# Where two modulation units stand beside the dense expert rows, and when their sums are taken

## The chip, the cores and the metric

The kernel runs on one core of one Trainium2 chip. Its time is the device time of that core in microseconds (us). Before the change three runs took 1870.52, 1871.92 and 1872.52 us, a median of 1871.92. A core has five engines that run side by side, each in the order of its own list of instructions: PE (matrix products), DVE (elementwise work on vectors), ACT (activations, copies and casts), POOL (here mostly the issue of gathers) and SP (here the issue of DMA transfers). They wait for one another by semaphores.

## The reference, cut to what matters

One layer over 512 tokens of 1024 values: a modulated norm, a token mixer, a second modulated norm, and a product-key mixture of 16384 experts (PEER).

```python
mod = (cond @ ada_w[l] + ada_b[l])[:, None, :]             # 6 vectors of 1024
sh1, sc1, gt1, sh2, sc2, gt2 = jnp.split(mod, 6, axis=-1)
...                                                        # token mixer, x = x + gt1 * y
h = rmsnorm(x, norm2_g[l]) * (1.0 + sc2) + sh2
x = x + gt2 * peer(h, peer_wq[l], peer_subkeys[l], peer_u[l], peer_v[l])
return rmsnorm(x, final_g)

# in peer, for each token: the 128 (expert, gate) pairs of its eight heads, then
ue = jnp.take(u_tab, experts, axis=0)
ve = jnp.take(v_tab, experts, axis=0)
act = jax.nn.gelu(jnp.einsum('pd,phkd->phk', xb, ue), approximate=False) * gate
return jnp.einsum('phk,phkd->pd', act, ve)
```

The last modulation vector, `gt2`, is used only at the very end, when the sum over the experts is scaled and added to x.

## The kernel before, in words

The modulation product is cut into 12 units of 512 output columns, two for each vector. `ada_unit(u)` loads the 1024 x 512 weights of one unit in four transfers of 512 KB (tile `adaw`), and DVE adds the eight row blocks, each times its 128 values of the condition, into `adac` (128 x 512, one operation at L152 and seven at L158). The sum over the 128 partitions is one PE product with a matrix of ones (L167), which takes one of the two PSUM banks named `hg`; DVE adds the bias row `adar` (loaded at L165) and a store sends the row to DRAM (`g2d`). Units 10 and 11 are the two halves of `gt2`.

The experts are computed in two ways. For 368 of the 512 tokens every expert is computed: this is the dense part, and it bounds the last half of the program. For the rest, 16 + 128 steps gather 1 MB of expert rows each by indirect DMA (POOL, L1175), and for each step DVE makes a dot product (L1188) and, after a small Gelu on ACT (L1192), an accumulation into `acc` or `accx` (L1183).

The dense part goes over 128 rows of 128 experts. Products are made in three passes of split numbers: a float32 tile `raw` of 512 KB is loaded, ACT casts its high part `whi` (L1020), DVE subtracts it to give the low part `wlo` (L1021), and PE makes lo x hi, hi x lo and hi x hi (L209 to L211).

- `scores(i)`: splits row i of u (`in_ut`), makes 24 products into a bank `hg`, and ACT takes the Gelu (L1034) into the ring `ga`. The first 32 rows are made earlier in the program and parked in DRAM; they come back as `gr`.
- `value_parts(i)`: splits row i of v (`in_uv`), multiplies `ga` or `gr` by the gates on DVE (L1156), casts the high part `ah` on ACT (L1158) and makes the low part `al` on DVE (L1159). `ah` and `al` have two buffers, for even and odd rows.
- `value_sum`: 18 products of row i into the accumulators `y`.

`dense()` runs over rows 0 to 125: the value part of row i, its 18 products, then from row 29 on `scores(i + 3)`, so that PE makes 18 products a row up to row 28, and 18 and 24 in turn after that. Behind rows 8 and 16 it calls `ada_unit`. The tiles `raw` and `adaw` share four buffers. `dense()` and `gather_all()` are generators that `run` advances in turn; from what they emit, a scheduler in the build sets the order of every engine by its own model of their times. At run time the engines keep that order.

Two tiles of a kind are told apart below by the number behind the name.

Of the kernel before, what the change touches and what calls it, by code (L numbers as in the profile page):

```python
# [68 lines left out]
def mixer_peer_kernel(ctx: ExitStack, tc: tile.TileContext, x, ws, ada, wba, vecs, rows, skt, uv, ut, out, dbg=None):  # L69
    nc = tc.nc  # L70
# [16 lines left out]
    def bank(tag):  # L87
        return (psh if tag == "hg" else ps).tile([P, 512], F32, tag=tag, name=tag, bufs=psb[tag])
# [4 lines left out]
    def w2(tag, shape=(P, 2, 256), dt=F32, bufs=1, name=None):  # L93
        pool = wka if tag in WKA else wkb if tag in WKB else wk
        return pool.tile(list(shape), dt, tag=tag, name=name or tag, bufs=bufs)
# [19 lines left out]
    ones = cst.tile([P, P], F32, name="ones")  # L115
# [21 lines left out]
    def ada_unit(u, first=False, pool=None):  # L137


        def work(name):  # L140
            return w2("ac", (P, 512), bufs=2, name=name) if pool is None else pool.tile([P, 512], F32, tag=name, name=name)

        pp = bank("tr") if pool is None else None
        acc = work("adac")
        parts = []
        for i in range(4):
            w = st.tile([P, 2, 512], F32, tag="raw", name="adaw")
            nc.sync.dma_start(w, ada[u, :, 2 * i:2 * i + 2])
            for a in range(2):
                kk = 2 * i + a  # L150
                if kk == 0:
                    nc.vector.tensor_scalar(acc, w[:, 0, :], cond[:, 0:1], None, op0=ALU.mult)  # L152
                elif first and a:
                    p = w2("gs", (P, 512), bufs=NGS, name="adap")
                    nc.scalar.mul(p, w[:, a, :], cond[:, kk:kk + 1])
                    parts.append(p)
                else:
                    nc.vector.scalar_tensor_tensor(acc, w[:, a, :], cond[:, kk:kk + 1], acc,  # L158
                                                   op0=ALU.mult, op1=ALU.add)
        parts.append(acc)  # L160
        if u // 2 in (2, 5):
            dst, o = (g1d, RW_B1) if u < 6 else (g2d, RW_B2)
            k = u % 2 * 512
            r = work("adar")
            nc.sync.dma_start(r, bass.AP(tensor=rows.tensor, offset=rows.offset + o + k, ap=[[0, P], [1, 512]]))  # L165
            pp = bank("hg") if pp is None else pp
            nc.tensor.matmul(pp, ones, acc, start=True, stop=True)  # L167
            nc.vector.tensor_add(r, r, pp)
            nc.sync.dma_start(dst[:, k:k + 512], r)
            return  # L170
        for n, p in enumerate(parts):
            for c in range(4):
                nc.tensor.matmul(pp[:, c * P:(c + 1) * P], p[:, c * P:(c + 1) * P], ones, start=n + c == 0,
                                 stop=n == len(parts) - 1, skip_group_check=True)
        m = mod[:, 4 * u:4 * u + 4]
        nc.vector.tensor_add(m, pp.rearrange("p (c n) -> p c n", c=4)[:, :, 0],
                             vec[:, VC_ADAB + 4 * u:VC_ADAB + 4 * u + 4])
        if u // 2 in (1, 4):
            dst, g = (a1, VC_N1) if u < 6 else (a2, VC_N2)
            k = u % 2 * 4  # L180
            nc.vector.scalar_tensor_tensor(dst[:, k:k + 4], m, 1.0, vec[:, g + k:g + k + 4], op0=ALU.add, op1=ALU.mult)
# [617 lines left out]
    def ada_rest():  # L799
        for u in range(4, 10):  # L800
            ada_unit(u)
            yield
# [128 lines left out]
    for u in (2, 0):  # L931
        ada_unit(u, True)
    for i in range(PRE):
        early[U_K, i] = half_unit(U_K, i)
    for u in (3, 1):
        ada_unit(u, True)
# [89 lines left out]
    def scores(i):  # L1026

        uh, ul = split_load(ut[i])
        o = bank("hg")
        for kk in range(KD):  # L1030
            c = slice(kk * P, (kk + 1) * P)
            mm3(o[:, :ND], uh[:, c], ul[:, c], dhi[:, kk, :], dlo[:, kk, :], kk == 0, kk == KD - 1)
        a = den.tile([P, ND], F32, tag="ga", name="ga", bufs=RING)
        nc.scalar.activation(a, o[:, :ND], AF.Gelu)  # L1034
        ga_ring[i] = a
# [86 lines left out]
    d3 = ctx.enter_context(tc.tile_pool(name="d3", bufs=1, **RT))  # L1122
# [19 lines left out]
    def value_parts(i):  # L1142
        vh, vl = split_load(uv[i * P:(i + 1) * P, D:2 * D])
        if i % 8 == 0:
            g = d3.tile([P, ND // 16, 8, 16], F32, tag="g", name="g", bufs=2)
            for b in range(GB if i == 0 else 1):
                q = slice(8 * b, min(8 * b + 8, ND // 16)) if i == 0 else slice(0, ND // 16)
                nc.sync.dma_start(g[:, q], gd[:, q, i:i + 8, :])
            gtile[0] = g
        if i < AHEAD:  # L1150
            a = den.tile([P, ND], F32, tag="gr", name="gr", bufs=BACK)
            nc.sync.dma_start(a, sd[i])
        else:
            a = ga_ring.pop(i)
        a3 = a.rearrange("p (q t) -> p q t", t=16)
        nc.vector.tensor_mul(a3, a3, gtile[0][:, :, i % 8, :])  # L1156
        ah, al = ahl[i % 2]
        nc.scalar.copy(ah[:, 0:ND], a)  # L1158
        last["lo"] = nc.vector.tensor_sub(al[:, 0:ND], a, ah[:, 0:ND])  # L1159
        return ah, al, vh, vl  # L1160

    def value_sum(i, b, hf, ah, al, vh, vl):
        c = slice(b * P, (b + 1) * P)
        d = slice(hf * 512, hf * 512 + 512)
        return mm3(yacc[b][:, d], ah[:, c], al[:, c], vh[:, d], vl[:, d], i == 0, i == P - 1)
# [49 lines left out]
    def dense():  # L1215
        for i in range(P - NEND):
            v = value_parts(i)
            for b in range(GB):
                for hf in range(2):
                    value_sum(i, b, hf, *v)  # L1220
            if AHEAD <= i + LEAD < P:
                scores(i + LEAD)
            if i in (8, 16):
                ada_unit(10 + i // 16, pool=d3)
            if i >= AHEAD - LEAD or i % 2:
                yield
            if i >= AHEAD - LEAD and i % 7 in (0, 2, 5):
                yield
# [14 lines left out]

    ga_ = gather_all()
    run(dense(), ga_)
    run(ga_)
    gf = d3.tile([P, 2 * D], F32, tag="rows", name="gf", bufs=NROWS)
# [66 lines left out]
```

## Time and profile before

| | |
|---|---|
| median of 3 runs | 1871.92 us |
| the profiled execution | 1871.05 us |
| its span, first to last instruction | 1869.3 us |
| granted TensorE clock, mean over the span | 0.990 of full |
| PE products | 1815.7 us busy, 97% |
| DVE | 1595.9 us busy, 85% |
| ACT | 934.9 us busy, 50% |
| POOL | 439.7 us busy, 24% |
| DMA | 473.63 MB, mean 253 GB/s |

The busy time of an engine is the time in which its instructions run; the span is that of the program. The rows further down come from four views: busy time by windows (each engine's busy us and number of instructions in a stretch, then the granted clock, the DMA engines' busy share and GB/s), sums of waits (which instruction waited for which, us in total, how often, the longest), and timelines of single engines (start, duration, instruction, tiles out and in; in brackets the idle time before it and what ended that). Instructions of one engine overlap a little, so the price of one in a row of several is the distance between two starts, not its printed duration.

### The profile page before, as it was taken

The page shows a single profiled execution, that of the slowest core. Times are in us where ns is not written, and L with a number is a line of the kernel's source. Part 1 is how long each engine was busy: PE and PEld are TensorE (multiplying, and loading weights), DVE is VectorE, ACT ScalarE, POOL GpSimd, SP SyncE. Part 2 cuts the span into 40 slices and gives each one's busy share as a digit, 9 for nine tenths or more (in the row PEclk, how much of TensorE's full clock was granted, in tenths as well). Part 3 has the DMA queues.
Part 4 walks back from the last instruction along what each step waited for, and adds up shares of the span by engine and source line. Part 5 has one row for each costly group of instructions (what it writes and reads, how often), then busy time and mean ns, then how long its engine had stood idle before and what let it go on. Part 6 is the DMA issues. An engine that isn't in the chain of part 4 may idle for free.

```text
span 1869.3 us, 31386 instructions
## 1 busy us (share of the span) xinstructions
PE 1815.7 (97%) x11421; PEld 1680.2 (90%) x11421; DVE 1595.9 (85%) x3478; ACT 934.9 (50%) x1735; POOL 439.7 (24%) x445
## 2 busy tenths in 40 slices
PE   7999989999999899999999999999999999999997
PEld 6999978999998899999877889889889889889886
DVE  6889966989999979999887768888888888888886
ACT  6778644676655677766433333333333333333332
POOL 1000000000000698887001112222212212122210
PEclk9999998999999999999999999999999999999999
DMA  9655744543355555666999969989998998999883
GB/s 317 183 182 186 230 143 133 177 132 94 117 168 173 171 183 200 219 219 254 325 337 332 351 230 352 337 306 349 340 334 307 351 345 308 343 333 327 327 304 113
DMA packets 161146, 473.63 MB, mean 253 GB/s; under 512 B 13280, under 2 KB 76896, under 8 KB 139616
## 3 DMA queue, kind: packets, MB, share of 16 engines
q1 hardware_dynamic: 140256, 320.63, 51.1%
q0 software_dynamic: 20736, 151.00, 21.2%
q8 instruction: 90, 1.47, 0.3%
q14 instruction: 64, 0.52, 0.1%
HBM read 436.18 MB, written 35.39 MB: 252 GB/s over the span
## 4 chain that ended last, share of the span: by engine, by line
PE 50%; DVE 1%; ACT 0%; issue 0%; DVEq 0%; POOLq 0%; POOL 0%; ACTq 0%
PE y L211 10%; PE y L210 10%; PE y L209 10%; PE hg L209 7%; PE hg L211 7%; PE hg L210 7%; DVE t L1212 0%; ACT ah L1158 0%; DVE al L1159 0%; DVE accx L1183 0%; DVE t L1205 0%; DVE t L1206 0%; DVE wlo L1021 0%; DVE rows L1188 0%; DVE gr L1156 0%
## 5 line engine op out<-in xcount | busy, mean ns | idle before, releaser
L1020 ACT CAST whi<-raw 128x1024 fp32r<-128x1024 f32 x256 | 267.2, 1045 | 260.3 <-PE y L211 231.4
L1021 DVE TENSOR_TENSOR wlo<-raw,whi 128x1024 fp32r<-128x1024 f32 x256 | 312.7, 1222 | 97.1 <-ACT whi L1020 96.9
L209 PE MATMUL hg<-dlo,whi 128*128 128x368 f32 x1024 | 339.7, 332 | 2.2 <-ACT ga L1034 2.2
L211 PE MATMUL hg<-dhi,whi 128*128 128x368 f32 x1024 | 338.8, 331 | 0.0
L210 PE MATMUL hg<-dhi,wlo 128*128 128x368 f32 x1024 | 338.4, 330 | 0.0
L1175 POOL DMA_INDIRECT rows<-in_uv,ei x128 | 168.4, 1315 | 595.1 <-DVE acc L1183 537.2
L211 PE MATMUL y<-whi,ah 128*128 128x512 f32 x768 | 305.7, 398 | 0.0
L210 PE MATMUL y<-whi,al 128*128 128x512 f32 x768 | 305.6, 398 | 0.1
L209 PE MATMUL y<-wlo,ah 128*128 128x512 f32 x768 | 298.1, 399 | 1.1 <-DVE wlo L1021 1.1
L1055 POOL TENSOR_SCALAR oj<-iof,tj 128x128 f32<-128x128 f32 x248 | 215.4, 885 | 42.3 <-PE gd L1068 30.2
L205 DVE TENSOR_TENSOR wlo<-raw,whi 128x1024 fp32r<-128x1024 f32 x160 | 194.8, 1219 | 33.5 <-ACT whi L204 33.4
L204 ACT CAST whi<-raw 128x1024 fp32r<-128x1024 f32 x160 | 167.3, 1048 | 91.7 <-PE pj L211 61.5
L209 PEld LDWEIGHTS hg<-dlo,whi 128*128 128x128 f32 x1024 | 192.3, 188 | 7.2 <-ACT ga L1034 2.5
L210 PEld LDWEIGHTS hg<-dhi,wlo 128*128 128x128 f32 x1024 | 192.5, 188 | 4.2
L1034 ACT ACTIVATE ga<-hg 128x368 f32<-128x368 f32 x128 | 60.8, 476 | 263.1 <-PE hg L211 256.4
L211 PEld LDWEIGHTS hg<-dhi,whi 128*128 128x128 f32 x1024 | 192.2, 188 | 0.0
L211 PEld LDWEIGHTS y<-whi,ah 128*128 128x128 f32 x768 | 145.4, 189 | 35.4
L209 PEld LDWEIGHTS y<-wlo,ah 128*128 128x128 f32 x768 | 144.9, 189 | 33.2 <-DVE wlo L1021 1.9
L210 PEld LDWEIGHTS y<-whi,al 128*128 128x128 f32 x768 | 145.5, 189 | 32.1 <-DVE al L1159 0.4
L1188 DVE SCALAR_TENSOR_TENSOR rows<-rows,h2g 128x1024 f32<-128x1024 f32 x128 | 153.1, 1218 | 0.0
L209 PE MATMUL pj<-wlo,hh 128*128 128x256 f32 x448 | 128.8, 287 | 4.8 <-ACT gsig L629 2.1
L211 PE MATMUL pj<-whi,hh 128*128 128x256 f32 x448 | 128.1, 286 | 0.0
(814 smaller groups left out, 3872.1 us busy)
## 6 DMA issues: line engine op xcount, KB each, us to landing
raw<-in_ws SPq DMA_DIRECT2D x160, 512.0 KB
raw<-in_ut SPq DMA_DIRECT2D x128, 512.0 KB
raw<-in_uv SPq DMA_DIRECT2D x128, 512.0 KB
adaw<-in_ada SPq DMA_DIRECT2D x48, 512.0 KB
gd<-stage SPq DMA_DIRECT2D x23, 1024.0 KB
g<-gd SPq DMA_DIRECT2D x15, 1472.0 KB
sd<-ga SPq DMA_DIRECT2D x32, 184.0 KB
gr<-sd SPq DMA_DIRECT2D x32, 184.0 KB
```

The source lines that it names most:

```text
L204: nc.scalar.copy(hi, w)
L205: nc.vector.tensor_sub(lo, w, hi)
L209: nc.tensor.matmul(o, lh, rl, start=start, stop=False, **kw)
L210: nc.tensor.matmul(o, ll, rh, start=False, stop=False, **kw)
L211: return nc.tensor.matmul(o, lh, rh, start=False, stop=stop, **kw)
L1020: nc.scalar.copy(hi, w)
L1021: nc.vector.tensor_sub(lo, w, hi)
L1034: nc.scalar.activation(a, o[:, :ND], AF.Gelu)
L1055: (nc.gpsimd if a < npool else nc.vector).tensor_scalar(oj4[:, a, :], iof, tj[:, t0 + a:t0 + a + 1], None, op0=ALU.is_equal)
L1175: nc.gpsimd.indirect_dma_start(out=r[c], out_offset=None, in_=uv, in_offset=bass.IndirectOffsetOnAxis(ap=ei[:, c:c + 1], axis=0))
L1188: dot = nc.vector.scalar_tensor_tensor(u, u, 1.0, h2, op0=ALU.mult, op1=ALU.mult, accum_out=s)
```

## The change

Units 10 and 11 are called behind dense rows 40 and 56 instead of 8 and 16. For these two units `ada_unit` no longer makes the sum over the partitions; it returns a function that does, and `dense()` calls that function four rows later, behind rows 44 and 60, with a bank taken there. The loads, the eight DVE operations and the sums are the same in kind and number.

```diff
             r = work("adar")
             nc.sync.dma_start(r, bass.AP(tensor=rows.tensor, offset=rows.offset + o + k, ap=[[0, P], [1, 512]]))
-            pp = bank("hg") if pp is None else pp
-            nc.tensor.matmul(pp, ones, acc, start=True, stop=True)
-            nc.vector.tensor_add(r, r, pp)
-            nc.sync.dma_start(dst[:, k:k + 512], r)
+
+            def sum_up(pp):
+                nc.tensor.matmul(pp, ones, acc, start=True, stop=True)
+                nc.vector.tensor_add(r, r, pp)
+                nc.sync.dma_start(dst[:, k:k + 512], r)
+
+            if pool is not None:
+                return sum_up
+            sum_up(pp)
             return
...
-            if i in (8, 16):
-                ada_unit(10 + i // 16, pool=d3)
+            if i in (40, 56):
+
+                sums = ada_unit(10 + i // 56, pool=d3)
+            if i in (44, 60):
+                sums(bank("hg"))
```

The scheduler sets the order anew. PE's list is the same but for the two sums, POOL's is the same, and ACT's, DVE's and SP's lists differ from about dense row 7 on. Line numbers from L167 on are five higher in the kernel after the change.

ACT before, around dense row 17. `whi_12446` is the high part of row 17's v; `gr_12450` and `gr_12487` are the factors of rows 17 and 18:

```order
L1158 CAST ah1_11845<-gr_12450 128x368
L1192 ACTIVATE gg__12478<-gs__12476 128x1
L1158 CAST ah0_11843<-gr_12487 128x368
L1020 CAST whi_12446<-raw_12444 128x1024
L1020 CAST whi_12483<-raw_12481 128x1024
```

ACT after the change, at the same place. `whi_12400` is the high part of row 17's v; `gr_12375` and `gr_12404` are the factors of rows 16 and 17:

```order
L1163 CAST ah1_11845<-gr_12336 128x368
L1025 CAST whi_12400<-raw_12398 128x1024
L1197 ACTIVATE gg__12364<-gs__12362 128x1
L1163 CAST ah0_11843<-gr_12375 128x368
L1025 CAST whi_12437<-raw_12435 128x1024
L1163 CAST ah1_11845<-gr_12404 128x368
```

The cast of row 17's v moved from behind the cast of row 18's factor to ahead of that of row 16's.

ACT before, around dense row 57. `whi_14835` is the high part of row 57's v, `whi_14786` that of row 59's u; `ga_14669` and `ga_14745` are the Gelus of rows 57 and 58:

```order
L1034 ACTIVATE ga_14669<-hg_14644 128x368
L1020 CAST whi_14786<-raw_14784 128x1024
L1192 ACTIVATE gg__14822<-gs__14820 128x1
L1192 ACTIVATE gg__14830<-gs__14828 128x1
L1020 CAST whi_14835<-raw_14833 128x1024
L1158 CAST ah1_11845<-ga_14669 128x368
L1034 ACTIVATE ga_14745<-hg_14720 128x368
```

ACT after the change, around dense row 57. `whi_14831` is the high part of row 57's v; `ga_14722` and `ga_14792` are the Gelus of rows 58 and 59:

```order
L1039 ACTIVATE ga_14722<-hg_14697 128x368
L1163 CAST ah0_11843<-ga_14722 128x368
L1197 ACTIVATE gg__14962<-gs__14960 128x1
L1197 ACTIVATE gg__14970<-gs__14968 128x1
L1039 ACTIVATE ga_14792<-hg_14767 128x368
L1025 CAST whi_14831<-raw_14829 128x1024
L1025 CAST whi_14858<-raw_14856 128x1024
```

The cast of row 57's v moved from ahead of row 58's Gelu to behind row 59's. In PE's list, before and after alike, the 24 products of row 59's scores (`hg_14767` after) stand directly ahead of the 18 products of row 57.

DVE before, around dense row 57. `ga_14669` is row 57's factor, `wlo_14836` the low part of row 57's v, `wlo_14787` that of row 59's u:

```order
L1156 TENSOR_TENSOR ga_14669<-ga_14669,g_14761 128x368
L1021 TENSOR_TENSOR wlo_14787<-raw_14784,whi_14786 128x1024
L1193 TENSOR_TENSOR gg__14822<-gg__14822,gate_10666 128x1
L1193 TENSOR_TENSOR gg__14830<-gg__14830,gate_10666 128x1
L1183 SCALAR_TENSOR_TENSOR acc_13193<-rows_14671,gg__14822,acc_13193 128x1024
L1183 SCALAR_TENSOR_TENSOR acc_13193<-rows_14679,gg__14830,acc_13193 128x1024
L1021 TENSOR_TENSOR wlo_14836<-raw_14833,whi_14835 128x1024
L1159 TENSOR_TENSOR al1_11846<-ga_14669,ah1_11845 128x368
```

DVE after the change, around dense row 57. `ga_14792` is row 59's factor, `wlo_14832` the low part of row 57's v:

```order
L1161 TENSOR_TENSOR ga_14792<-ga_14792,g_14738 128x368
L158 SCALAR_TENSOR_TENSOR adac_14794<-adaw_14807,cond_104,adac_14794 128x512
L1188 SCALAR_TENSOR_TENSOR acc_13147<-rows_14813,gg__14962,acc_13147 128x1024
L158 SCALAR_TENSOR_TENSOR adac_14794<-adaw_14807,cond_104,adac_14794 128x512
L1188 SCALAR_TENSOR_TENSOR acc_13147<-rows_14821,gg__14970,acc_13147 128x1024
L1026 TENSOR_TENSOR wlo_14832<-raw_14829,whi_14831 128x1024
L1026 TENSOR_TENSOR wlo_14859<-raw_14856,whi_14858 128x1024
```

Ahead of the subtraction for row 57 there now stand row 59's factor and the last two `adac` operations of the second unit, with two accumulations between them.

DVE before, around dense row 41. `wlo_13715` is the low part of row 44's u, `ga_13597` row 42's factor:

```order
L1159 TENSOR_TENSOR al1_11846<-ga_13529,ah1_11845 128x368
L1188 SCALAR_TENSOR_TENSOR rows_13599,gs__13748<-rows_13599,h2g_7598 128x1024
L1156 TENSOR_TENSOR ga_13597<-ga_13597,g_13613 128x368
L1021 TENSOR_TENSOR wlo_13715<-raw_13712,whi_13714 128x1024
L1193 TENSOR_TENSOR gg__13750<-gg__13750,gate_10666 128x1
```

DVE after the change, around dense row 41. `wlo_13688` is the low part of row 44's u, `ga_13621` row 43's factor:

```order
L1161 TENSOR_TENSOR ga_13621<-ga_13621,g_13567 128x368
L1198 TENSOR_TENSOR gg__13799<-gg__13799,gate_10666 128x1
L158 SCALAR_TENSOR_TENSOR adac_13623<-adaw_13636,cond_104,adac_13623 128x512
L1188 SCALAR_TENSOR_TENSOR acc_13147<-rows_13642,gg__13791,acc_13147 128x1024
L1026 TENSOR_TENSOR wlo_13688<-raw_13685,whi_13687 128x1024
```

The subtraction for row 44's scores moved behind row 43's factor and the last `adac` operation of the first unit.

## Rows read from the trace of the kernel before

**Rows 1.** Windows: us, then busy us (instructions) by engine, clock, DMA share, GB/s
```profile
921.90:994.40 72.50, 72.50 (x309) 57.81 (x308) 59.89 (x93) 25.22 (x39) 6.07 (x5) 1.00 0.95 325
994.40:1005.60 11.20, 8.45 (x22) 5.88 (x22) 7.85 (x12) 3.55 (x4) 1.20 (x1) 0.70 0.99 360
1052.60:1848.10 795.50, 795.50 (x4052) 714.95 (x4051) 656.06 (x924) 291.10 (x522) 168.96 (x129) 1.00 0.87 320
```

**Rows 2.** Sums of waits of PE, 921.8 to 1848 us
```profile
PE hg L167 <- DVE adac L158: 1.7, 1, 1.7
PE y L209 <- DVE wlo L1021: 1.1, 1, 1.1
```

**Rows 3.** Timeline of PE around the products of row 17
```profile
994.21 0.39 PE L211 MATMUL y<-whi,ah 128*128 128x512 f32 x1
996.27 1.12 PE L167 MATMUL hg<-adac,ones 128*128 128x512 f32 x2 [1.67 <-DVE adac L158]
998.48 0.79 PE L209 MATMUL y<-wlo,ah 128*128 128x512 f32 x1 [1.08 <-DVE wlo L1021]
...
1004.89 0.40 PE L209 MATMUL y<-wlo,ah 128*128 128x512 f32 x1
...
1005.59 0.39 PE L209 MATMUL y<-wlo,ah 128*128 128x512 f32 x1
```

**Rows 4.** Timeline of PE, first products of a row and of the scores behind
```profile
1201.25 0.39 PE L209 MATMUL y<-wlo,ah 128*128 128x512 f32 x1
...
1205.47 0.33 PE L209 MATMUL hg<-dlo,whi 128*128 128x368 f32 x1
```

**Rows 5.** Timeline of PE at the first unit's sum
```profile
959.85 1.02 PE L167 MATMUL hg<-adac,ones 128*128 128x512 f32 x2
960.30 1.27 PE L209 MATMUL y<-wlo,ah 128*128 128x512 f32 x3
```

**Rows 6.** Timeline of ACT around row 17
```profile
995.72 0.50 ACT L1158 CAST ah<-gr 128x368 fp32r<-128x368 f32 x1 [2.79 <-DVE gr L1156]
996.12 1.04 ACT L1020 CAST whi<-raw 128x1024 fp32r<-128x1024 f32 x1
```

**Rows 7.** Timeline of DVE around row 17
```profile
985.35 0.75 DVE L158 SCALAR_TENSOR_TENSOR adac<-adaw,cond,adac 128x512 f32<-128x512 f32 x1
986.01 1.28 DVE L1183 SCALAR_TENSOR_TENSOR accx<-rows,gg__12387,accx 128x1024 f32<-128x1024 f32 x1
987.21 0.75 DVE L158 SCALAR_TENSOR_TENSOR adac<-adaw,cond,adac 128x512 f32<-128x512 f32 x1
...
995.02 0.53 DVE L1156 TENSOR_TENSOR gr<-gr,g 128x368 f32<-128x368 f32 x1
995.47 0.74 DVE L158 SCALAR_TENSOR_TENSOR adac<-adaw,cond,adac 128x512 f32<-128x512 f32 x1
...
997.20 1.22 DVE L1021 TENSOR_TENSOR wlo<-raw,whi 128x1024 fp32r<-128x1024 f32 x1
```

**Rows 8.** Timeline of ACT at the row that begins at 1201.25
```profile
1201.45 0.48 ACT L1034 ACTIVATE ga<-hg 128x368 f32<-128x368 f32 x1 [2.57 <-PE hg L211]
```

**Rows 9.** Timeline of DVE at the row that begins at 1201.25
```profile
1201.96 0.54 DVE L1156 TENSOR_TENSOR ga<-ga,g 128x368 f32<-128x368 f32 x1 [0.62 <-ACT ga L1034]
```

**Rows 10.** Windows of 10 us in which PE goes on after a wait
```profile
653.80:663.80 10.00, 8.35 (x44) 6.62 (x44) 9.10 (x30) 7.20 (x21) 9.85 (x15) 0.86 0.64 236
998.50:1008.50 10.00, 10.00 (x31) 7.90 (x32) 5.63 (x9) 2.19 (x5) 0.00 (x0) 0.69 0.95 337
915.60:925.60 10.00, 7.85 (x40) 7.16 (x41) 9.93 (x19) 3.20 (x5) 0.00 (x0) 1.00 0.91 352
```

**Rows 11.** Timeline of PE, a wait ahead of the dense part
```profile
917.75 0.43 PE L209 MATMUL hg<-dlo,whi 128*128 128x368 f32 x1 [2.16 <-ACT ga L1034]
```

**Rows 12.** Sums of ACT's waits for loads, 921.8 to 1848 us
```profile
ACT whi L1020 <- DMA raw<-in_uv: 8.0, 7, 2.0
ACT whi L1020 <- DMA raw<-in_ut: 6.3, 4, 2.8
```

## The prediction

> **What bounds the kernel now.** I read the windows of the second half first, then the sums of PE's waits there, then the timelines of PE, ACT and DVE around the longest wait. From 921.9 us to 1848 us PE is busy in 72.50 of 72.50 us, then in 8.45 of 11.20, and in 795.50 of the last 795.50 [rows 1]: the dense part goes as fast as PE does. A change of work on other engines or queues counts only where it makes PE wait, takes a wait away, or moves the clock. The sums of waits hold just two, one of 1.7 and one of 1.1 us [rows 2], and both lie at row 17, where the second unit's sum and the low part of row 17's v are late [rows 3].
>
> **What the wait of row 17 costs.** The last product of row 16 begins at 994.21 and the last three of row 17 at 1004.89, the next product at 1005.59: 11.38 us [rows 3]. Without waits, at the full clock, one product takes 4.22 / 18 = 0.2345 us (18 of them from 1201.25 to 1205.47 [rows 4]), the sum 0.45 us (959.85 to 960.30 [rows 5]), and row 17's products 4.22 us: 4.90 in all. So 11.38 - 4.90 = 6.48 us are lost. Of these, 2.89 are the clock: 15 products from 998.48 to 1004.89 took 6.41 us, 0.427 each, where 15 x 0.2345 = 3.52 is the full speed; the granted clock of the stretch is 0.70 [rows 1, 3], and its low part is the level of 1.2 GHz. The other 3.59 are waiting.
>
> Why PE waited is read backwards. Its first product needs `wlo`, begun on DVE at 997.20; that needs ACT's cast `whi`, begun at 996.12, right behind a cast `ah` at 995.72 that had waited 2.79 us for a multiplication on DVE [rows 6, 7]. The order of ACT says that this `ah` is row 18's and stands ahead of row 17's `whi`; the multiplication it waits for stood on DVE behind accumulations and `adac` operations of the second unit [rows 7].
>
> **The change part by part.**
>
> *Rows 8 to 28 without the units.* ACT's new order has row 17's `whi` ahead of row 16's factor, so a late factor no longer delays v, and the `adac` operations are gone from this stretch. The first term is -6.48 us. Bounds: not more, since PE has no other wait there [rows 2]; nothing, if the rows from 9 on were bound by transfers instead (the DMA share is 0.95 and 0.99 there [rows 1]), which is a rival below. I take it whole, as the 4 x 512 KB of each unit leave this stretch too.
>
> *The sums.* They cost PE 0.45 us each, at rows 44 and 60 as at 8 and 17, so nothing is added. The `adac` chain has four rows of 8.24 us to end, and the bank that a sum takes is free once a Gelu of 0.48 us [rows 8] is over, while 18 products (4.22 us [rows 4]) run. If that cover were gone it would cost about 0.5 us; I take 0. The bias load, addition and store hang on nothing that PE waits for. On SP the four loads now stand among those of rows 40 to 60 and on DVE the eight operations of 0.66 us (985.35 to 986.01 [rows 7]) likewise, about 5 us a unit, in windows where DVE is busy 656.06 of 795.50 us [rows 1]: hidden as work, except where order makes it late, as follows. POOL's order does not change.
>
> *Row 57, the second unit.* This is the step on which the forecast rests. Before, row 57's v is cast on ACT ahead of row 58's Gelu, more than a row early. Now it stands behind row 59's Gelu, and that Gelu waits for the 24 products that end just where PE wants to start row 57. On DVE the subtraction stands behind row 59's multiplication, which waits for the same Gelu, and behind four long operations. Counted from the end of the scores' products: in the row that starts at 1201.25, DVE's multiplication behind the Gelu begins at 1201.96, 0.71 later [rows 4, 9]. Then the distances between starts: multiplication 0.45 (995.02 to 995.47), `adac` 0.66 (985.35 to 986.01), accumulation 1.20 (986.01 to 987.21), `adac` 0.66, accumulation 1.20, and from `wlo`'s start to PE's first product 1.28 (997.20 to 998.48) [rows 3, 7]. Sum: 0.71 + 0.45 + 0.66 + 1.20 + 0.66 + 1.20 + 1.28 = 6.16 us of PE idle. ACT's own chain is shorter: Gelu 0.20 behind the end (1201.25 to 1201.45) and 0.48 long, `whi` 1.04, then 1.28: 3.0 us [rows 3, 4, 6 to 8]. DVE keeps its order, so 6.16 is taken and 3.0 is the low end. Behind the subtraction on DVE stands that of row 60's u; PE needs it only after row 57's 18 products, so it adds nothing.
>
> *The clock behind that wait.* Windows of 10 us with a restart have a granted clock of 0.86, 0.69 and, in one case, 1.00 [rows 10]. With two levels, the time at 1.2 GHz is 20 x (1 - clock): 2.8, 6.2 and 0 us. A microsecond at the low level loses (0.427 - 0.2345) / 0.427 = 0.45 us, so the cost is 1.3, 2.8 (2.89 measured above) or 0. An idle of 2.16 us left the clock at full [rows 10, 11], but the present one would be nearly three times as long and longer than that of row 17. I take the middle of 1.3 and 2.8, 2.1 us, and keep 0 and 2.9 as ends. The Trainium skill ("TensorE: Matmul & The Clock Gate", Part 1, the HAM clock gate) says that 1.2 GHz is the state that PE falls back to when idle and that it must be kept busy for a while before it runs at 2.4 GHz again; by it the cost would be sure, between the 1.3 and the 2.9 of the rows, and the case without any would not occur, whereas the wait that ended at 917.75 did go without.
>
> *Row 41, the first unit.* The low part of row 44's u stands on DVE behind row 43's multiplication (0.71 after the start of row 41's products), 0.45, an `adac` 0.66, an accumulation 1.20, and takes 1.28 to reach PE: 4.30 us against the 4.22 us that row 41's products last [rows 4, 7, 9]. So there is no slack left, and anything late shows. Four loads of `adaw` take the same four buffers as `raw`, so the loads behind them start only when DVE has used them up; ACT's waits for loads elsewhere were 11 in number, 14.3 us in total, 1.3 on average, 2.8 at the longest [rows 12]. Bounds 0 and 2.8; I take 0.3.
>
> **Sum.** -6.48 + 6.16 + 2.1 + 0.3 = +2.1 us, made against the profiled execution (1871.05: the span 1869.3 and 1.75 around it), which lies 0.87 below the median of the runs, 1871.92. Against that median the forecast is 1874.0 us: the stall is not removed but moved from row 17 to row 57, and it is a little longer there.
>
> **Rivals.**
>
> 1. *The clock stays at full behind row 57.* For it speaks the wait that ended at 917.75; against it, that this idle is longer. Time: -6.48 + 6.16 + 0 + 0 = -0.3, 1871.6 us.
>
> 2. *Row 41 waits as well* (the slower side). The four `adaw` loads hold the buffers, the load of row 44's u or row 41's v lands late, and PE waits the longest that a raw load was waited for, 2.8, and pays its own clock of 2.1: 4.9 instead of 0.3, so +6.7 and 1878.6 us. It decides from about half a microsecond of lateness, since row 41 has no slack. Against it: the ring of scores runs three rows ahead, and the average wait of 1.3 us was on ACT alone and never reached PE in this part.
>
> 3. *Nothing is won at row 17*, because the rows before 29 are bound by loads (a row takes 4.22 us of PE and needs 0.5 MB of v and its gathers; the share is 0.95 to 0.99 [rows 1]). Then the stall comes back in another shape: +2.1 + 6.48 = +8.6, 1880.5 us. Against it: at 0.95 to 0.99 PE had no other wait there [rows 1, 2], and 4 MB of `adaw` go.
>
> 4. *Row 57 waits only for ACT's chain*, 3.0 us, and the clock stays: -6.48 + 3.0 = -3.5, 1868.4 us. This would need DVE's four long operations out of the way, as if `wlo` passed them; the chain of row 17 shows DVE in its order [rows 7], which speaks against it.
>
> **How the numbers follow.** A change of under 0.2%, 3.74 us, can't be told from none by a measurement of this kernel. The forecast has 0.50 (0.44 within that bound, 0.06 above it, where the clock takes 2.9 and row 41 over a microsecond), rival 1 has 0.11 (within), rival 2 has 0.21 (slower), rival 3 has 0.05 (slower), rival 4 has 0.13 (0.07 faster, 0.06 within, as -3.5 lies at the bound). So faster 0.07, within 0.61, slower 0.32. The forecast's own range is 1871.0 to 1877.5: from no loss to the clock with the runs' scatter of about a microsecond below, to 2.9 for the clock and 2.8 at row 41 above. The range for 8 in 10 reaches on to rival 2 and part of rival 4: 1869.5 to 1879.0, which leaves out rival 3, most of rival 4 and the tails.
>
> **What the profile after would show.** Rows 8 to 28: PE without a wait and the granted clock at 1.00; a wait for `whi`, `wlo` or a load of v there speaks for rival 3. Row 57: one PE wait of 5.5 to 6.5 us, `y` on `wlo`, ended by DVE, with the two `adac` and two accumulations between row 59's multiplication and `wlo`; a wait near 3 us would be rival 4, none at all would mean that the order is not what decides. Behind it products at 0.43 us for 3 to 6 us, or at 0.2345 throughout (rival 1). Row 41: a PE wait of under 0.5 us, `hg` on `wlo`; over 2 us, with ACT waiting for a load, is rival 2. The sums at rows 44 and 60 with no idle ahead of them. The forecast is wrong as a whole if PE shows no wait of over 3 us at row 57.

## The result and the profile after

The change made the kernel slower: 1886.14 us (median of four runs, 1883.61 to 1890.84) against 1871.36 us; the ratio of the runs is 1.0086 with a 95% interval of 1.0071 to 1.0101 (the medians alone give 1.0079). Forecast were 1874.0 us and a range to 1879.0.

The profiled execution took 1890.84 us and is the slowest of the four. A line of its page (busy time of each engine, share of the span, instructions):

```profile
PE 1821.5 (96%) x11421; PEld 1684.4 (89%) x11421; DVE 1594.8 (84%) x3478; ACT 935.1 (50%) x1735; POOL 442.5 (23%) x445
```

Row 0 of the dense part begins at 928.17 us in it and began at 921.89 before, yet the lists of the engines agree up to there and on to about row 7. Two kernels of the experiments have these same lists up to row 0, and in their profiles it began at 918.82 and 922.72. So these 6.28 us are scatter of the lead-in, and I compare from row 0 on: from the first product of row 0 to that of row 125 it took 922.08 us before and 935.94 after, 13.86 more. With the profiled execution before, 1871.05 + 13.86 = 1884.9, close to the new median.

Where they lie is read from the starts of rows on PE's timeline (us; row 29 is the first with scores behind it):

| kernel | rows 0 to 8 | 8 to 29 | 29 to 56 | 56 to 58 | 58 to 125 |
|---|---|---|---|---|---|
| before | 33.74 | 97.01 | 222.77 | 16.48 | 552.08 |
| after | 33.74 | 99.60 | 223.70 | 25.96 | 552.94 |

Two stretches by windows: from the start of row 8 to that of row 28, before and after, and the two rows 56 and 57 after (columns as in [rows 1]).

```profile
955.60:1047.80 92.20, 89.45 (x366) 70.52 (x365) 75.03 (x112) 32.42 (x51) 11.13 (x10) 0.96 0.96 346
```

```profile
961.90:1056.60 94.70, 89.29 (x361) 70.54 (x360) 67.35 (x100) 30.66 (x50) 10.03 (x10) 0.95 0.84 292
1285.20:1311.20 26.00, 18.70 (x86) 16.31 (x86) 21.24 (x34) 6.62 (x12) 6.09 (x5) 0.87 0.92 345
```

In that first stretch, where the units were taken out, the DMA share fell from 0.96 to 0.84, DVE's busy time from 75 to 67 us, and the rows still got longer. PE's waits from row 0 on, which answer to [rows 2]:

```profile
PE y L214 <- DVE wlo L1026: 7.3, 1, 7.3
PE y L215 <- DVE al L1164: 5.4, 3, 3.2
```

**The wait for v at row 17 is gone, but rows 11 and 15 wait for `al`.** PE after the change at row 11: its first line is three products of `wlo` and `ah`, the second the first product that needs `al`, the last belongs to row 12:

```profile
974.71 0.86 PE L214 MATMUL y<-wlo,ah 128*128 128x512 f32 x3
978.79 0.80 PE L215 MATMUL y<-whi,al 128*128 128x512 f32 x1 [3.22 <-DVE al L1164]
979.39 0.63 PE L216 MATMUL y<-whi,ah 128*128 128x512 f32 x1
...
984.91 0.86 PE L214 MATMUL y<-wlo,ah 128*128 128x512 f32 x3
```

Row 11 takes 10.20 us instead of 4.22, with products at 0.427 us behind the wait. Row 15 has 1.82 us of waiting and takes 3.6 more, row 21 0.6 more. DVE at row 11 shows why. In the order of its lines: `al` of row 10, the multiplications of row 13 (970.86) and of row 14 (977.74), and only then `al` of row 11:

```profile
970.41 0.54 DVE L1164 TENSOR_TENSOR al<-gr,ah 128x368 fp32r<-128x368 f32 x1
970.86 0.54 DVE L1161 TENSOR_TENSOR gr<-gr,g 128x368 f32<-128x368 f32 x1
...
977.74 0.54 DVE L1161 TENSOR_TENSOR gr<-gr,g 128x368 f32<-128x368 f32 x1 [5.21 <-DMA gr<-sd]
978.20 0.54 DVE L1164 TENSOR_TENSOR al<-gr,ah 128x368 fp32r<-128x368 f32 x1
```

The issues of `gr` on SP, and the gather that POOL issued just before one of them:

```profile
970.98 0.32 SPq L1157 DMA_DIRECT2D gr<-sd  x1
...
978.76 0.32 SPq L1157 DMA_DIRECT2D gr<-sd  x1
```

```profile
970.77 0.99 POOL L1180 DMA_INDIRECT rows<-in_uv,eix  x1 [10.83 <-DVE accx L1188]
```

`gr` has four buffers, so row 14's load can be issued only when `al` of row 10, begun at 970.41, is done. It is issued at 970.98, 0.2 us behind a gather of 1 MB, and DVE gets it at 977.74. Behind DVE's wait stands `al` of row 11, for which PE waits. Before the change DVE's list there read so (`gr_12293` is row 13, `gr_12227` row 11, `gr_12330` row 14), with `al` of row 11 ahead of row 14's multiplication:

```order
L1156 TENSOR_TENSOR gr_12293<-gr_12293,g_12107 128x368
L1159 TENSOR_TENSOR al1_11846<-gr_12227,ah1_11845 128x368
L1188 SCALAR_TENSOR_TENSOR rows_12034,gs__12253<-rows_12034,h2x_7599 128x1024
L1021 TENSOR_TENSOR wlo_12290<-raw_12287,whi_12289 128x1024
L1156 TENSOR_TENSOR gr_12330<-gr_12330,g_12107 128x368
```

After it (`gr_12270` is row 13, `gr_12307` row 14, `gr_12204` row 11):

```order
L1161 TENSOR_TENSOR gr_12270<-gr_12270,g_12107 128x368
L1026 TENSOR_TENSOR wlo_12238<-raw_12235,whi_12237 128x1024
L1161 TENSOR_TENSOR gr_12307<-gr_12307,g_12107 128x368
L1164 TENSOR_TENSOR al1_11846<-gr_12204,ah1_11845 128x368
```

The waits of DVE for these loads, from row 0 to row 28, before and after:

```profile
DVE gr L1156 <- DMA gr<-sd: 0.2, 1, 0.2
```

```profile
DVE gr L1161 <- DMA gr<-sd: 24.5, 10, 5.2
```

Row 15 waits for another pair and another reason. On DVE the multiplication of row 17 stands ahead of `al` of row 15 and waits; before the change it stood behind it. On SP the load of the next eight rows' gates (`g`, 1.5 MB) is issued at 982.89. The issue behind it, of row 16's load, then lasts 7.73 us instead of 0.32, and row 17's load follows only at 991.65, though its buffer had been free since `al` of row 13 ended at 986.23. DVE, PE and SP there:

```profile
999.19 0.54 DVE L1161 TENSOR_TENSOR gr<-gr,g 128x368 f32<-128x368 f32 x1 [3.60 <-DMA gr<-sd]
999.64 0.53 DVE L1164 TENSOR_TENSOR al<-gr,ah 128x368 fp32r<-128x368 f32 x1
```

```profile
1000.24 0.50 PE L215 MATMUL y<-whi,al 128*128 128x512 f32 x1 [1.82 <-DVE al L1164]
```

```profile
982.89 0.37 SPq L1153 DMA_DIRECT2D g<-gd  x1
983.35 7.73 SPq L1157 DMA_DIRECT2D gr<-sd  x1
...
991.65 0.38 SPq L1157 DMA_DIRECT2D gr<-sd  x1
```

The place in the list alone makes no wait: row 15's multiplication stands ahead of `al` of row 12 as well, its load was there in time, and row 12 took its 4.22 us.

**Row 57 waits as forecast, 1.3 us longer.** PE's last product of the scores there, the first of row 57, and one behind it; then ACT and DVE:

```profile
1293.28 0.33 PE L216 MATMUL hg<-dhi,whi 128*128 128x368 f32 x1
1300.90 0.80 PE L214 MATMUL y<-wlo,ah 128*128 128x512 f32 x1 [7.30 <-DVE wlo L1026]
1301.50 0.63 PE L215 MATMUL y<-whi,al 128*128 128x512 f32 x1
```

```profile
1294.78 0.20 ACT L1197 ACTIVATE gg__14970<-gs__14968 128x1 f32<-128x1 f32 x1 [0.94 <-DVE rows L1193]
1294.89 0.46 ACT L1039 ACTIVATE ga<-hg 128x368 f32<-128x368 f32 x1
```

```profile
1293.51 1.22 DVE L1193 SCALAR_TENSOR_TENSOR rows<-rows,h2g 128x1024 f32<-128x1024 f32 x1
...
1295.46 0.53 DVE L1161 TENSOR_TENSOR ga<-ga,g 128x368 f32<-128x368 f32 x1
1295.92 0.74 DVE L158 SCALAR_TENSOR_TENSOR adac<-adaw,cond,adac 128x512 f32<-128x512 f32 x1
1296.58 1.28 DVE L1188 SCALAR_TENSOR_TENSOR acc<-rows,gg__14962,acc 128x1024 f32<-128x1024 f32 x1
1297.78 0.74 DVE L158 SCALAR_TENSOR_TENSOR adac<-adaw,cond,adac 128x512 f32<-128x512 f32 x1
1298.44 1.28 DVE L1188 SCALAR_TENSOR_TENSOR acc<-rows,gg__14970,acc 128x1024 f32<-128x1024 f32 x1
1299.63 1.22 DVE L1026 TENSOR_TENSOR wlo<-raw,whi 128x1024 fp32r<-128x1024 f32 x1
```

From row 59's multiplication on, every distance is the one of the forecast: 0.46, 0.66, 1.20, 0.66, 1.19, 1.27. From where row 57's products were due (1293.28 and one product of 0.17 us: 1293.45) to 1300.90 it is 7.45 us, against 6.16 in the forecast. The 1.3 us lie ahead of the multiplication: the Gelu of row 59 began 1.44 us behind PE and not 0.20, since a small Gelu of a gather stands ahead of it on ACT and waited for a dot product that DVE began only at 1293.51.

**A sum costs 0.86 us, not 0.45.** PE at the first sum after the change:

```profile
1193.71 1.02 PE L168 MATMUL hg<-adac,ones 128*128 128x512 f32 x2
1194.17 0.80 PE L214 MATMUL y<-wlo,ah 128*128 128x512 f32 x1
1194.81 0.40 PE L215 MATMUL y<-whi,al 128*128 128x512 f32 x1
```

It takes 0.46, and the product behind it 0.64 instead of 0.2345.

### The profile page after: what moved, and what is told of

It is laid out like the page before. It is cut to its first block, busy times and chain, and to the rows that moved or that the text cites. A ratio compares the mean times of both kernels' runs of the same rounds, so it can differ in the third digit from the quotient of the medians.

```text
span 1889.1 us, 31366 instructions
## 1 busy us (share of the span) xinstructions
PE 1821.5 (96%) x11421; PEld 1684.4 (89%) x11421; DVE 1594.8 (84%) x3478; ACT 935.1 (50%) x1735; POOL 442.5 (23%) x445
## 4 chain that ended last, share of the span: by engine, by line
PE 45%; DMA 3%; DVE 2%; issue 1%; ACT 0%; SPq 0%; DVEq 0%; POOLq 0%; POOL 0%
PE y L215 8%; PE y L216 8%; PE y L214 8%; PE hg L214 7%; PE hg L216 7%; PE hg L215 7%; DMA gr<-sd 2%; DMA raw<-in_ut 1%; DVE rows L1193 0%; DVE wlo L1026 0%; DVE al L1164 0%; DVE acc L1188 0%; DVE adac L158 0%; DVE t L1217 0%; DVE gr L1161 0%
## 5 line engine op out<-in xcount | busy, mean ns | idle before, releaser
L1180 POOL DMA_INDIRECT rows<-in_uv,ei x128 | 173.6, 1356 | 600.8 <-DVE acc L1188 544.7
```

Of the source, the lines that this page charges most:

```text
L1180: nc.gpsimd.indirect_dma_start(out=r[c], out_offset=None, in_=uv, in_offset=bass.IndirectOffsetOnAxis(ap=ei[:, c:c + 1], axis=0))
```

## The experiments

The theory (A) after the result: two separate waits, both made by order. In rows 8 to 28 DVE's multiplication of a row two or three further on (row 14 at row 11, row 17 at row 15) stands ahead of the `al` that PE needs, and its load is late; at row 57 the second unit's operations stand ahead of row 57's v. The main rival (B): these stretches are bound by their transfers or by the units' work, and the order only says where it shows. All kernels are edits of the changed one. The same cut of PE's timeline as above for all of them, each from one profiled execution; the ratios are to the kernel before, run beside each:

| kernel | rows 0 to 8 | 8 to 29 | 29 to 56 | 56 to 58 | 58 to 125 | ratio to before, interval |
|---|---|---|---|---|---|---|
| changed | 33.74 | 99.60 | 223.70 | 25.96 | 552.94 | 1.0086 (1.0071 to 1.0101) |
| rows alone | 34.13 | 98.42 | 223.61 | 27.11 | 552.08 | 1.0091 (1.0076 to 1.0105) |
| rule for DVE | 33.73 | 89.23 | 223.70 | 24.04 | 552.94 | 1.0022 (1.0012 to 1.0032) |
| rule for ACT | 33.74 | 100.68 | 223.75 | 20.51 | 552.93 | 1.0064 (1.0050 to 1.0077) |
| both rules | 33.73 | 89.30 | 223.70 | 21.91 | 552.94 | 1.0004 (0.9995 to 1.0013) |
| fifth buffer | 34.49 | 95.82 | 223.33 | 25.64 | 552.05 | 1.0035 (1.0024 to 1.0046) |
| 33 and 49, both rules | 33.74 | 89.22 | 224.96 | 16.48 | 552.08 | 0.9978 (0.9965 to 0.9990) |
| 32 and 48, both rules | 33.73 | 89.23 | 224.45 | 16.48 | 552.08 | 0.9983 (0.9975 to 0.9992) |
| 33 and 49, no rule | 33.73 | 99.96 | 224.56 | 16.48 | 552.08 | 1.0027 (1.0012 to 1.0042) |
| 33 and 49, rule for DVE | 33.74 | 89.23 | 224.55 | 16.48 | 552.08 | 0.9967 (0.9955 to 0.9979) |

Rows 8 to 28 repeat: the four kernels that have the changed order of multiplications and `al` there (changed, rows alone, rule for ACT, and 33 and 49 without a rule) took 98.42 to 100.68 us, the five with the rule for DVE 89.22 to 89.30.

**One half of the change alone: the rows, with the sums taken at once.**

```diff
-            if i in (44, 60):
+            if i in (40, 56):
                 sums(bank("hg"))
```

> The units stand beside rows 40 and 56, but their sums are taken at once, as before the change (one half of the change alone). Theory A (the order of the lists sets the waits; the moved units cost what they do at rows 11, 15 and 57, and the later sums little): rows 8 to 28 as after the change, with waits of y for al of 3.2 and 1.8 us; at row 56 the sum waits about 4 us for adac and row 57's v another 2.5, so that row 57 costs about what it does after the change; time within 3 us of the changed kernel's 1886.1. Rival B (the later sums are what costs, for they hold a bank of hg between the scores): about 1875, without the wait at row 57.

Measured: 1888.33 us (1880.93 to 1890.45). PE's waits from row 0 on:

```profile
PE y L215 <- DVE al L1164: 5.8, 2, 4.1
PE hg L168 <- DVE adac L158: 5.1, 1, 5.1
PE y L214 <- DVE wlo L1026: 1.9, 1, 1.9
```

The time can't be told from the changed kernel's. The wait at row 57 only has another name: now the sum waits for the last `adac`. So the later sums are not what costs; rival B of this run falls. The other half alone (rows 8 and 16 with the sums called at 12 and 20) was not run: the scheduler gives it the lists of the kernel before, instruction for instruction.

**A rule for DVE in rows under 32.**

```diff
+    los, his = {}, {}
...
-        nc.vector.tensor_mul(a3, a3, gtile[0][:, :, i % 8, :])
+        m = nc.vector.tensor_mul(a3, a3, gtile[0][:, :, i % 8, :])
+        if i < AHEAD and i - 2 in los:
+            behind(m, los[i - 2])
...
-        last["lo"] = nc.vector.tensor_sub(al[:, 0:ND], a, ah[:, 0:ND])
+        last["lo"] = los[i] = nc.vector.tensor_sub(al[:, 0:ND], a, ah[:, 0:ND])
```

> The changed kernel with one rule of order more: on DVE the multiplication of row i (i under 32) stands behind al of row i - 2. Nothing else is asked for; row 57 keeps its order. Theory A (rows 8 to 28 lose 10.2 us because the multiplication that waits for a late load of gr stands ahead of the al that PE needs next): the waits of y for al at rows 11 and 15 are gone, no wait of PE over 0.5 us in rows 8 to 28, the low clock behind them gone too; row 57 waits 6 to 7.5 us as now; time 10 us less than the changed kernel, about 1876. Rival B (these rows are bound by their transfers, and the order only says where PE waits): PE waits elsewhere in these rows for as long, for a v or an al, and the time stays at 1884 to 1888.

Measured: 1876.06 us (1870.86 to 1878.22). The stretch from row 0 to row 28 by windows, PE's only wait from row 0 on, and DVE's waits for `gr` in that stretch:

```profile
920.40:1038.50 118.10, 118.10 (x506) 94.97 (x505) 88.36 (x131) 44.82 (x69) 11.12 (x11) 1.00 0.88 303
```

```profile
PE y L214 <- DVE wlo L1026: 6.0, 1, 6.0
```

```profile
DVE gr L1162 <- DMA gr<-sd: 4.7, 2, 2.4
```

The same stretch of the changed kernel:

```profile
928.20:1056.60 128.40, 122.99 (x505) 97.63 (x504) 89.09 (x132) 44.34 (x69) 11.02 (x11) 0.96 0.82 278
```

With the rule PE is busy 118.10 of 118.10 us. The same loads, gathers and operations go through in 10.37 us less (99.60 to 89.23), at 303 GB/s instead of 278. Transfers did not bound these rows; rival B falls here. The lists of PE, ACT and POOL are those of the changed kernel; DVE's differs in the rows under 32, and SP's in ten places: loads of `gr` move ahead, most of them past the gates' loads. So at row 11 the order on DVE is what was mended; at row 15 the order on SP changed beside it. A late load is still there, behind the gates of row 16: DVE waits 2.4 us for row 18's, and PE does not.

Row 57's lists are the changed kernel's, yet it lost less. Its wait is close to the forecast's 6.16. PE's last product of the scores began at 1275.18, so row 57's products were due at 1275.35. ACT's Gelu began 0.20 us later, and row 57 itself 6.15 us later:

```profile
1275.55 0.48 ACT L1039 ACTIVATE ga<-hg 128x368 f32<-128x368 f32 x1 [0.42 <-PE hg L216]
```

```profile
1281.50 0.79 PE L214 MATMUL y<-wlo,ah 128*128 128x512 f32 x1 [6.00 <-DVE wlo L1026]
```

**A rule for ACT.** `last["hi"]` is the cast `whi` of row i's v; `behind` puts the cast `ah` of row i behind `whi` of row i - 1.

```diff
+        his[i] = last["hi"]
...
-        nc.scalar.copy(ah[:, 0:ND], a)
+        c = nc.scalar.copy(ah[:, 0:ND], a)
+        if i - 1 in his:
+            behind(c, his[i - 1])
```

> The changed kernel with another rule of order: on ACT the cast ah of row i stands behind the cast whi of row i - 1's v. Rows 9 to 18 on DVE keep the order of the changed kernel (the multiplication of row 14 ahead of al of row 11, for one); at row 57 the adac operations now stand ahead of the multiplication of row 59, and wlo of row 57 directly behind it. Theory A: the wait at row 57 falls from 7.3 to 2 to 3 us and the clock keeps up or loses up to 2; rows 11 and 15 wait as in the changed kernel, 2 to 5 us together with their clock; time about 1886 - 6 = 1880. Rival B (the second unit costs its DVE work and loads wherever it stands): row 57 or its neighbours still lose 6 us or more, time 1885 to 1887.

Measured: 1882.88 us (1880.60 to 1888.38). PE's longest waits from row 0 on, and DVE at row 57:

```profile
PE y L215 <- DVE al L1168: 6.6, 3, 3.7
PE y L214 <- DVE wlo L1026: 2.9, 1, 2.9
```

```profile
1290.31 0.54 DVE L1163 TENSOR_TENSOR ga<-ga,g 128x368 f32<-128x368 f32 x1 [2.58 <-ACT ga L1039]
1291.34 1.23 DVE L1026 TENSOR_TENSOR wlo<-raw,whi 128x1024 fp32r<-128x1024 f32 x1 [0.49 <-ACT whi L1025]
```

The scheduler now puts the `adac` operations on DVE ahead of row 59's multiplication, and `wlo` directly behind it. With them and the accumulations out of the way, row 57's wait is 2.9 us, about the 3.0 that the forecast gave for ACT's chain alone, and the two rows take 20.51 instead of 25.96. Rows 8 to 28, whose order of multiplications and `al` was left, still lose 11.5 us against 89.23, more than the 2 to 5 that were expected of rows 11 and 15. The two causes are separate.

**Both rules.**

> The changed kernel with both rules of order. Theory A: no wait over 0.5 us in rows 8 to 28, at row 57 one of 1 to 3 us; the time is that of the changed kernel less 10 and less 6 to 7, about 1869, at or a little under the kernel before (1871.4), whose row 17 lost 6.5 us. Rival B (loads bound rows 8 to 28; the second unit's work is on the path): 1880 or more.

Measured: 1872.16 us (1870.37 to 1877.55), the same as before the change, where about 1869 was expected. Rows 8 to 28 are free of waits; row 57 kept more than expected:

```profile
PE y L214 <- DVE wlo L1026: 3.6, 1, 3.6
```

ACT waited 0.7 us more there for the load of row 57's v, and rows 56 and 57 still take 5.43 us over 16.48.

**A fifth buffer for `gr`, with the blamed order.**

```diff
-BACK = 4
+BACK = 5
...
+        if i < AHEAD and i - 4 in los:
+            behind(m, los[i - 4])
```

> The changed kernel with five buffers for gr instead of four, and on DVE the multiplication of row i behind al of row i - 4, which leaves the multiplication of row 14 ahead of al of row 11, as in the changed kernel. So the order that is blamed stays there, but gr of row 14 may be loaded once al of row 9 is done, a row of 4.2 us earlier. Theory A (the load is late because it waits for the buffer that al of row i - 4 sets free): the waits of y for al of rows 11 and 15 (3.2 and 1.8 us) go or fall under 1.5, time 1876 to 1879, row 57 as in the changed kernel. Rival B (the order alone, whenever the load is issued): waits of 2 to 4 us at rows 11 to 16 remain, 1884 to 1887. Rival C (transfers bound these rows): the same time as B, with waits elsewhere.

Measured: 1876.50 us (1873.51 to 1886.14; the profiled execution is the slowest). The waits at rows 11 and 15 are gone, two others came, at row 14 (1.4 us) and row 22 (3.3). DVE ahead of row 22's wait, and its waits for `gr` up to row 28:

```profile
1025.21 0.54 DVE L1162 TENSOR_TENSOR gr<-gr,g 128x368 f32<-128x368 f32 x1 [5.37 <-DMA gr<-sd]
```

```profile
DVE gr L1162 <- DMA gr<-sd: 18.6, 7, 5.4
```

That is row 25's multiplication, ahead of `al` of row 22 in DVE's list; at row 14 it is row 17's. Both loads stand on SP behind the gates' loads of rows 16 and 24. The waits for loads that the four buffers made late are gone, though the scheduler now puts the multiplication of row i + 3 ahead of `al` of row i in all of rows 8 to 28 but row 23; the changed kernel has that at rows 9, 11, 12 and 21. So both the place in the list and the late load are needed for a wait, and a load can be late for its buffer or for what stands ahead of it on SP. Theory A's time came, its waits only in part. No run moved the gates' loads alone.

**Other rows for the units, with both rules.**

```diff
-            if i in (40, 56):
+            if i in (33, 49):
...
-            if i in (44, 60):
+            if i in (37, 53):
```

> Both rules of order (multiplication of row i behind al of row i - 2, ah of row i behind whi of row i - 1), and the units beside rows 33 and 49 instead of 40 and 56, sums four rows later. Theory A: the last wait of the kernel with both rules, 3.6 us at row 57 with its 1.7 of clock, came from where row 56's unit falls among the Gelu, the loads and the gathers, and is gone here; no wait of PE over 0.5 us from row 0 on; time that of both rules less 5, about 1867, 0.2 to 0.35% under the kernel before. Rival B (a unit costs its own 3 to 6 us wherever it stands): 1871 to 1873 with a wait at row 34 or 50.

Measured: 1867.27 us (1863.36 to 1874.45). The largest wait of PE from row 0 on is this:

```profile
PE hg L215 <- DVE wlo L1026: 0.2, 1, 0.2
```

So a unit costs PE little more than its sum when its place is good, and row 57's loss was that of the place.

> As the kernel with units beside rows 33 and 49 and both rules of order, but beside rows 32 and 48, so that each unit's loads stand next to the load of the gates of eight rows. Theory A: the same 1867 within 2 us, no wait over 1 us at rows 33 or 49. Rival B (the load of 1.5 MB of gates beside the unit's 2 MB holds the queue up): a wait of 2 us or more at rows 33 to 35 or 49 to 51 and 1870 or more.

Measured: 1867.72 us (1865.42 to 1872.53), with no wait of PE at all. The load of the gates beside a unit does no harm; rival B falls.

**The rows alone, and the rows with the rule for DVE alone.**

> The changed kernel with rows 33 and 49 in place of 40 and 56 and no rule of order: only two numbers differ. Rows 8 to 28 have the changed kernel's order on DVE, with the multiplication of row 14 ahead of al of row 11. Theory A (two separate causes): no wait at rows 50 to 62, but waits of y for al in rows 11 to 24 of 3 to 7 us in total, with their clock; time 1886 - 9.5 = 1877, 4 to 7 us over the kernel before. Rival B (one cause: moving the units is bad as such): 1883 or more with a wait beside the new rows. Rival C (the new rows alone explain the gain of the kernel with rows 33 and 49 and both rules): 1867 to 1869.

Measured: 1875.34 us (1871.88 to 1882.24). With nothing but the rows changed, row 57's loss is gone and that of rows 8 to 28 is all that is left:

```profile
PE y L215 <- DVE al L1164: 5.9, 3, 3.2
```

> Rows 33 and 49 with the one rule that keeps the multiplication of row i behind al of row i - 2 on DVE; ACT is left to the scheduler. Theory A: no wait over 0.5 us from row 0 on, 1867 as with both rules. Rival B (the rule on ACT is needed too): a wait of 2 us or more beside row 34 or 50 and 1870 or more.

Measured: 1864.21 us (1863.34 to 1866.28), ratio 0.9967 (0.9955 to 0.9979). The dense part by windows:

```profile
921.80:1837.90 916.10, 916.10 (x4565) 811.34 (x4564) 757.05 (x1077) 338.93 (x593) 184.04 (x140) 1.00 0.89 323
```

PE is busy throughout at the full clock. This version beats both kernels, the one before by 0.2 to 0.5%; the rule for ACT is not needed with these rows. From row 0 on it takes 916.08 us, the two versions with both rules 916.48 and 915.97, so the three can't be told apart there.

## Why the prediction was wrong

- **What bounds the kernel: right.** From row 0 on, every difference in time was a wait of PE, its clock, or a sum.
- **The loss at row 17: right.** With row 17 free, rows 16 and 17 together take 6.92 us less: the 6.48 and a sum.
- **"Rows 8 to 28 without the units", -6.48: the step that failed.** I took the whole gain and bounded the loss at nothing, because PE had no other wait there before and the units' work went. That argument holds for the load on the engines, not for their order, which the scheduler set anew. I had read ACT's new order at row 17, and not DVE's at rows 11 to 15, where a multiplication now stood ahead of an `al` due sooner and waited for a late load: at row 11 one that the four buffers release late, at row 15 one that SP issued late behind the gates' load. Those waits and their clock cost 10.37 us (99.60 against 89.23), so the term was 10.37 - 6.48 = +3.89 instead of -6.48. The trace of before could not show the wait itself: DVE waited 0.2 us for `gr` there.
- **Row 57, +6.16: right mechanism, a little small.** 7.45 us; the 1.3 missing are the late Gelu, a chain that ran from a dot product over ACT. With the same lists and a Gelu in time (the rule for DVE) it was 6.15. The rule for ACT and the other rows each took the larger part of it away or all of it.
- **The clock there, +2.1: right.** Products from 1300.90 on ran at 0.43 us, and of the 9.48 us that rows 56 and 57 grew by, 2.03 are left beside the 7.45. Rival 1 (the clock stays at full) did not come: the granted clock of the window is 0.87. The Trainium skill ("TensorE: Matmul & The Clock Gate", Part 1, the HAM clock gate) has the low level as the default, which activity releases. Here the trace agrees.
- **Row 41, +0.3, and rival 2: no wait.** Rows 41 and 42 lost 0.09 us.
- **The sums, 0: nearly right as a difference, wrong in size.** Each costs 0.86, before as well, but there the second was hidden in part in row 17's wait, so 0.4 were added. All together: 3.89 + 7.45 + 2.03 + 0.09 + 0.4 is the 13.86 us from row 0 on.
- **Rival 3 came nearest in time (1880.5), by the wrong cause.** It asked whether loads bound rows 8 to 28 by their volume; the rule for DVE shows that they do not.

Still open: why a `gr` load, once issued, takes longer in one place than in another. Row 14's, issued 0.2 us behind a gather, was there 6.76 us later. A gather alone does not explain it: row 20's was issued 0.21 us behind one as well (1004.78), and DVE used it 4.40 us later without a wait. No run took the gathers away.

## What to carry to other kernels

When a scheduler sets the order anew, compare the whole list of each engine over the stretch that lost work, not only at the wait that should go: look for an instruction that waits for a late load and has something urgent behind it. Look also at what stands ahead of that load on the engine that issues it: a buffer that comes free early is of no use while the issue is held up. A short wait on DVE or ACT that costs nothing where it stands becomes PE's own when the next instruction in its list is the one that PE needs. And a rule of order of a few lines, which keeps such a pair apart, was worth 11 us here (1875.34 to 1864.21), as much as the choice of place itself (1886.14 to 1875.34).

## What the runs showed of the hardware that was not expected

The sum, a 128x512 product of float32 tiles among products of split ones, cost nearly twice its own time: 0.46 us, and 0.64 instead of 0.2345 for the product right behind it; rows 8 and 9 before the change, and 44, 45, 60 and 61 after it, are 0.85 to 0.86 us longer in pairs. On SP the issue right behind the 1.5 MB load of the gates took 7.73 us in the changed kernel, where others take 0.32. And the lead-in of the same lists (before, changed, rows alone, and 33 and 49 without a rule) took between 918.8 and 928.2 us to row 0, more scatter than most of the effects studied here, so profiles are compared from a common instruction on.
